# Another order for the side work of the query and key units in an encoder block

## The chip, the core and the metric

The kernel runs on one core of a Trainium2 chip. The time is the device time of one execution in microseconds (us). A core has a matrix engine (TensorE, PE in the profile), three engines for element-wise work (VectorE or DVE, ScalarE or ACT, GpSimd or POOL) and SyncE (SP), whose queue starts most of the transfers here. Each engine works through its own queue in order and waits, where it has to, for semaphores that others set.

## The reference, cut to what matters

One layer of an encoder, all in float32, with 256 tokens and a width of 2048:

```python
h = _rmsnorm(x, norm1_g)
proj = h @ w_in                 # q: 12 heads of 128, k and v: 4 heads of 128, u: 512
a = _rmsnorm(_window_attention(q, k, v, sink), attn_out_g)
f = _rmsnorm(_fourier_mix(u, w_fourier), fourier_out_g)
x = x + jnp.concatenate([a, f], axis=-1) @ w_out
x = x + _conv_ffn(_rmsnorm(x, norm2_g), w_up, dw_w, dw_b, w_down)
return _rmsnorm(x, normf_g)
```

In the attention, a head's scores are `q k^T` times a constant, plus a term that falls with the distance of the two tokens; `m` is the larger of the greatest score and the head's sink, `p = exp(scores - m)` is divided by its sum (with the sink in it), and the result multiplies `v`. Three query heads share one key head.

## The kernel before, in words

**Precision by parts.** Each product is made of three: a float32 operand is split into a high part (`hi`, rounded to the matrix engine's format) and the rest (`lo`). For weights that come from memory, ACT makes `hi` (L181) and DVE makes `lo` (L182), 128 x 2048 numbers at a time. Activations are split in the same way, mostly by `split_scaled` (ACT L269, DVE L270).

**Units.** The work up to the output projection is a row of units, each with one such piece of weights: units 4 to 7 make v, units 8 to 23 make q and k (16 units in groups of four: k, then three q; one has 32 matmuls at L350), units 24 to 39 are the output projection. The function `unit` sets the order in every queue for unit i:

1. `before`: small matmuls of other heads (values L749, turned weights L704, scores L654), on PE ahead of the unit's own;
2. the unit's own matmuls, on PE;
3. `beside`: the side work on ACT, DVE, POOL and SP, the part that is changed;
4. `split(i + 2)`: the split of weights (L181, L182) for the unit after the next, and on SP the load of weights three pieces ahead;
5. `behind`: the exponentials (`exps`, ACT L684 and L688, then a sum on POOL, L689).

Nothing but the order of these calls and the semaphores decides what runs when. In this document "the `lo` of unit i" is the L182 at the end of unit i's side work, which holds weights of unit i + 2.

**The way of a head.** Let a q head be made by unit s. Its steps fall into later units:

- s + 1: `qk_out` reads the two halves of the product from PSUM and adds them (ACT `tmp` L631, DVE `add` L633; for a k, one more DVE step, L635). `qk_parts` splits the sum into the parts `qT` or `kT` (ACT L269 or L643, DVE L270 or L644).
- s + 2: on PE `scores` (L654), first in the unit. Then `scores_out` adds the distances and takes the maxima (DVE L670); POOL makes `neg` out of the maxima in two steps on 128 x 2 numbers (L674, L675). Behind the split, `exps`.
- s + 3: `weigh` divides by the sum (DVE, reciprocal L694, scaling L697), and `flip_out` transposes 32 x 32 blocks (DVE L314) and sends them to memory (SP L317). The last two heads have no flip; PE turns their weights (L704) in s + 4, and `turn_out` splits them (L716, L717).
- s + 4: `flip_in` reads the blocks back in turned order (SP L325).
- s + 6: `flip_parts` splits the turned weights into `pt` (ACT L739, DVE L740, two halves each).
- s + 7 (s + 5 without a flip): on PE `values` (L749), first in the unit; `values_out` squares the head's output (ACT L486), splits it into `cat` (L269, L270) and adds the squares on POOL (L490).

So one unit's side work belongs to as many as five heads. Heads are made only by the q units, so that the work repeats every four units. Counted from unit 8: the first and second unit of a group (16 and 17, 20 and 21) have all steps; the second has a k to sum; the third (18, 22) has no scores and no turned weights to split; the fourth (19, 23) has no scaling, transposition or values.

Of the kernel before, what the change touches and what calls it, by code (L numbers as in the profile page):

```python
# [55 lines left out]
FLIPS = range(NH - 2)  # L56
# [48 lines left out]
def block_kernel(  # L105
# [30 lines left out]
    def bank(pool, name):  # L136
        return pool.tile([P, 512], F32, tag=pool.name, name=name)
# [79 lines left out]
    def u_part(k, o, n, m=1):  # L217

        rows = ux[k // 4][:, (k < 4) * U_HEAD :].rearrange("p (k c) -> p k c", k=4)
        return rows[:, k % 4 : k % 4 + m, o : o + n]  # L220
# [39 lines left out]
    ps = bank(dn, "ps_warm")  # L260
# [112 lines left out]
    before, beside, behind = {}, {}, {}  # L373

    def at(when, i, f, *a):
        when.setdefault(i, []).append((f, a))
# [17 lines left out]
    for k in range(NK):  # L394
# [3 lines left out]
        n = 1 if c < 2 else 2  # L398
# [3 lines left out]
        if q % n == 0:  # L402
            w, h = u_part(k, 0, FW, n), hi[:, q : q + n, :]
# [222 lines left out]
    qk_sb, st = {}, {}  # L626
    sq_a = ph.tile([P, S], F32, tag="sq", name="sq_a")

    def qk_out(kind, h, ps):
        tmp = ph.tile([P, S], F32, tag="tmp", name=f"tmp_{kind}{h}", bufs=2)  # L630
        nc.scalar.activation(tmp, ps[:, S : 2 * S], AF.Copy)  # L631
        add = ph.tile([P, S], F32, tag="add", name=f"add_{kind}{h}", bufs=2)
        nc.vector.tensor_tensor(add, ps[:, 0:S], tmp, ALU.add)  # L633
        if kind == "k":
            nc.vector.tensor_tensor(add, add, r1b, ALU.mult)  # L635
        st["add", kind, h] = add
# [125 lines left out]
    for i in range(N_QK, N_OUT + 8):  # L762
        heads = {i - s: h for (kind, h), s in slot_of.items() if kind == "q"}
        new = [kh for kh, s in slot_of.items() if i - s == 1]
        for n, h in sorted(heads.items()):
            if n == 5 + 2 * (h in FLIPS):
                at(before, i, values, h)
        if 4 in heads and heads[4] not in FLIPS:
            at(before, i, turn, heads[4])
        if 2 in heads:  # L770
            at(before, i, scores, heads[2])
        if 6 in heads and heads[6] in FLIPS:
            at(beside, i, flip_parts, heads[6])
        if 3 in heads:
            at(beside, i, weigh, heads[3])
            if heads[3] in FLIPS:
                at(beside, i, flip_out, heads[3])
        if 4 in heads and heads[4] in FLIPS:
            at(beside, i, flip_in, heads[4])
        for kind, h in new:  # L780
            at(beside, i, lambda k=kind, h=h: qk_out(k, h, st.pop(("ps", k, h))))
        for n, h in sorted(heads.items()):
            if n == 5 + 2 * (h in FLIPS):
                at(beside, i, values_out, h)
        if 4 in heads and heads[4] not in FLIPS:
            at(beside, i, turn_out, heads[4])
        if 2 in heads:
            at(beside, i, scores_out, heads[2])
        for kind, h in new:
            at(beside, i, qk_parts, kind, h)  # L790
        if 2 in heads:
            at(behind, i, exps, heads[2])

# [85 lines left out]
    for n, (c, kq) in enumerate(OUT_ORDER):  # L879
        i = N_OUT + n  # L880
# [14 lines left out]
        if kq >= 2:  # L895
            part = "a" if kq == 2 else "f"
            ps = ps_a[c] if kq < 3 else ps_a[c, "f"]
# [315 lines left out]
    for q in range(2):  # L1213
        kind, j = items[q]
        ps = bank(mm, f"ps_{kind}{j}")
# [15 lines left out]
    for n, it in enumerate(items):  # L1231
# [8 lines left out]
        if it[0] in ("gate", "val"):  # L1240
            kind, j = it
            ps = bank(mm, f"ps_{kind}{j}")
# [4 lines left out]
        if it[0] == "product":  # L1247
            kind, g, c, p = it
# [3 lines left out]
            elif end and p in ("P2", "N4"):  # L1252
                ps = joined[c, p] = bank(mm, f"ps_{p}{g}{c}")
                by_parts(ps, parts[p], *halves.pop(it), GROUPS[g][1], True, False)
            else:
                ps = bank(mm, f"ps_{p}{g}{c}")
# [5 lines left out]
        else:  # L1262
            kind, c = it
            hi, lo = halves.pop(up_index[n])
            if c < 2:
                ps = [joined.pop((c, p)) for p in ("P2", "N4")]
            else:
                ps = [bank(mm, f"ps_l{c}{b}") for b in range(2)]
# [10 lines left out]
    i = up_index[n]  # L1279
# [158 lines left out]
```

## Time and profile before

| | |
|---|---|
| median of 3 runs | 940.92 us (940.85 to 941.05) |
| the profiled execution | 941.03 us, of which span 938.9 us |
| busy: TensorE, DVE, ACT, POOL | 928.0, 765.5, 539.6, 72.9 us |
| mean granted clock of TensorE | 0.997 |
| the q and k units, by TensorE | about 53 to 157 us of the span |

A row of a timeline has the start in us from the span's start, the duration in us, the engine, the line of the kernel, the operation, what it writes from what it reads, and in brackets how long the engine had been idle before it and what released it. A row of the waits has the engine and line that waited, the engine and line waited for, and the total in us, the number of times and the longest. Names have their numbers left out: `lo` is every low part of weights.

### The profile page before, as it was taken

To read this page: it belongs to the slowest core of one execution; us is meant where nothing else is said; L and a number is where in the kernel's file an instruction comes from. 1 tells how busy PE (TensorE), PEld (TensorE's weight loads), DVE (VectorE), ACT (ScalarE), POOL (GpSimd) and SP (SyncE) were. 2 spreads that over 40 slices of the span, in tenths; PEclk is the share of its full clock that TensorE was granted. 3 is DMA by queue.
4 is the path that set the end of the run, shared out by engine and by line. 5 is a ranking of instruction groups with operands and counts; after the bars stand their busy time and mean duration, and the time that the engine had idled before them with its cause. 6 is when DMAs were issued, how large, how long until landed. Compare 5 with 4: busy or idle time off the path is not lost.

```text
span 938.9 us, 12849 instructions
## 1 busy us (share of the span) xinstructions
PE 928.0 (99%) x5005; PEld 803.5 (86%) x5005; DVE 765.5 (82%) x945; ACT 539.6 (57%) x672; POOL 72.9 (8%) x104
## 2 busy tenths in 40 slices
PE   9999999999999999999999999999999999999996
PEld 7888888888888888888888888888888888888885
DVE  7657888778677777798888997878979789989986
ACT  7755666645554555566555665556655556655553
POOL 0102222300000000000000000000000000000002
PEclk9999999999999999999999999999999999999998
DMA  9965767557757668887797778777787978779652
GB/s 367 309 224 169 231 196 236 193 174 281 243 221 232 177 227 238 278 269 239 220 296 252 246 216 286 237 262 232 260 248 240 309 224 269 241 233 273 194 179 90
DMA packets 55148, 223.25 MB, mean 238 GB/s; under 512 B 21136, under 2 KB 25744, under 8 KB 31536
## 3 DMA queue, kind: packets, MB, share of 16 engines
q1 hardware_dynamic: 50544, 192.94, 56.8%
q0 software_dynamic: 4544, 29.49, 16.9%
q8 instruction: 39, 0.64, 0.3%
q14 instruction: 21, 0.17, 0.1%
HBM read 216.13 MB, written 6.29 MB: 237 GB/s over the span
## 4 chain that ended last, share of the span: by engine, by line
PE 95%; DVE 2%; ACT 1%; issue 1%; DMA 0%; POOL 0%; DVEq 0%; POOLq 0%; ACTq 0%
PE ps_val L350 25%; PE ps_gate L350 25%; PE ps_q L350 5%; PE ps_P L1148 3%; PE ps_P L1149 3%; PE ps_P L1147 3%; PE ps_N L1148 3%; PE ps_N L1149 3%; PE ps_N L1147 3%; PE ps_k L350 2%; PE ps_a L333 2%; PE ps_a L335 2%; PE ps_a L334 2%; PE ps_s L654 1%; PE ps_ff L333 1%; PE ps_ff L335 1%
## 5 line engine op out<-in xcount | busy, mean ns | idle before, releaser
L182 DVE TENSOR_TENSOR lo<-raw,hi 128x2048 fp32r<-128x2048 f32 (+1 forms) x129 | 293.5, 2275 | 53.9 <-ACT hi L181 53.6
L181 ACT ACTIVATE hi<-raw 128x2048 fp32r<-128x2048 f32 (+1 forms) x129 | 245.3, 1902 | 36.7 <-PE ps_a L334 14.6
L350 PE MATMUL ps_val<-hU,hi 128*128 128x512 f32 x688 | 236.2, 389 | 0.0
L350 PE MATMUL ps_gate<-hU,hi 128*128 128x512 f32 x688 | 236.2, 389 | 0.0
L350 PE MATMUL ps_val<-hU,lo 128*128 128x256 f32 x688 | 189.9, 276 | 0.0
L350 PE MATMUL ps_gate<-hU,lo 128*128 128x256 f32 x688 | 189.9, 276 | 0.0
L350 PEld LDWEIGHTS ps_gate<-hU,hi 128*128 128x128 f32 x688 | 129.1, 188 | 26.8
L350 PEld LDWEIGHTS ps_val<-hU,hi 128*128 128x128 f32 x688 | 129.1, 188 | 26.8
L350 PEld LDWEIGHTS ps_gate<-hU,lo 128*128 128x128 f32 x688 | 129.1, 188 | 1.3
L350 PEld LDWEIGHTS ps_val<-hU,lo 128*128 128x128 f32 x688 | 129.1, 188 | 1.3
L922 ACT ACTIVATE ft_g<-ps_gate 128x256 f32<-128x256 f32 x43 | 16.5, 384 | 123.0 <-PE ps_gate L350 123.0
L922 ACT ACTIVATE ft_v<-ps_val 128x256 f32<-128x256 f32 x43 | 16.5, 384 | 91.5 <-PE ps_val L350 91.5
L350 PE MATMUL ps_q<-hT,hi 128*128 128x512 f32 x192 | 65.1, 391 | 0.0
L1147 PE MATMUL ps_P<-hi_P,op_P 128*128 128x512 f32 x144 | 56.0, 389 | 0.0
L1148 PE MATMUL ps_P<-hi_P,op_P 128*128 128x512 f32 x144 | 56.0, 389 | 0.0
L1149 PE MATMUL ps_P<-lo_P,op_P 128*128 128x512 f32 x144 | 56.0, 389 | 0.0
L350 PE MATMUL ps_q<-hT,lo 128*128 128x256 f32 x192 | 51.2, 277 | 0.0
L1039 DVE TENSOR_TENSOR lo_N<-sumw,hi_N 128x2048 fp32r<-128x2048 f32 (+1 forms) x20 | 41.5, 2077 | 9.4 <-ACT hi_N L1038 9.2
L1147 PE MATMUL ps_N<-hi_N,op_N 128*128 128x512 f32 x108 | 42.0, 389 | 0.0
L1148 PE MATMUL ps_N<-hi_N,op_N 128*128 128x512 f32 x108 | 42.0, 389 | 0.0
L1149 PE MATMUL ps_N<-lo_N,op_N 128*128 128x512 f32 x108 | 42.0, 389 | 0.0
L350 PEld LDWEIGHTS ps_q<-hT,hi 128*128 128x128 f32 x192 | 35.2, 188 | 6.6
(389 smaller groups left out, 1598.9 us busy)
## 6 DMA issues: line engine op xcount, KB each, us to landing
raw<-in_w_up SPq DMA_DIRECT2D x86, 1024.0 KB, 5.6
raw<-in_w_in SPq DMA_DIRECT2D x20, 1024.0 KB, 5.3
raw<-in_w_out SPq DMA_DIRECT2D x16, 1024.0 KB, 4.9
sumw<-in_w_down POOLq DMA_DIRECT2D x16, 1024.0 KB, 8.7
raw<-in_w_down_late SPq DMA_DIRECT2D x4, 1024.0 KB, 7.0
raw<-in_w_down_last SPq DMA_DIRECT2D x4, 768.0 KB, 4.2
turnp<-flip SPq DMA_DIRECT2D x40, 64.0 KB, 2.9
flop<-turnp SPq DMA_DIRECT2D x10, 256.0 KB, 4.7
```

The lines of the kernel that those rows point to most:

```text
L181: nc.scalar.activation(hi[:, 0:n], raw[:, 0:n], AF.Copy)
L182: nc.vector.tensor_tensor(lo[:, 0:n], raw[:, 0:n], f32(hi[:, 0:n]), ALU.subtract)
L333: nc.tensor.matmul(ps, ah, wh, start=first and q == q0, stop=False)
L334: nc.tensor.matmul(ps, al, wh, start=False, stop=False)
L335: nc.tensor.matmul(ps, ah, wl, start=False, stop=last and q == q0 + len(kk) - 1)
L350: nc.tensor.matmul(ps[:, x], (hi, lo)[i][:, k * P : (k + 1) * P], hk(k)[:, x], start=n == 0 and k == 0, stop=n == len(order) - 1 and k == ...
L654: nc.tensor.matmul(ps[:, b * S : (b + 1) * S], qT[:, qo + b * P : qo + (b + 1) * P], kT[:, ko : ko + S], start=n == 0, stop=n == 2,)
L922: nc.scalar.activation(tmp, ps[:, S : 2 * S], AF.Copy)
L1039: nc.vector.tensor_tensor(lo, src, f32(hi), ALU.subtract)
L1147: nc.tensor.matmul(ps, o[:, 0, p, :], hi[:, s], start=first and p == 0, stop=False)
L1148: nc.tensor.matmul(ps, o[:, 1, p, :], hi[:, s], start=False, stop=False)
L1149: nc.tensor.matmul(ps, o[:, 0, p, :], lo[:, s], start=False, stop=last and p == n - 1)
```

## The change

Before, the order of a unit's `beside` was: turned weights split, scaling and transposition, transposed blocks read back, sum of the new q or k, a head's output, (turned weights of the last two heads,) scores, parts of the new q or k. After, it is: sum of the new q or k, turned weights split, its parts, a head's output, scaling and transposition, transposed blocks read back or turned weights of the last two heads, scores. On each engine the queue holds the same instructions as before in the new order; the split of weights and the exponentials still follow. In units without a new q or k (25 on) only a head's output changes its place, to stand ahead of the scaling.

```diff
         if 2 in heads:
             at(before, i, scores, heads[2])
+        for kind, h in new:
+            at(beside, i, lambda k=kind, h=h: qk_out(k, h, st.pop(("ps", k, h))))
         if 6 in heads and heads[6] in FLIPS:
             at(beside, i, flip_parts, heads[6])
+        for kind, h in new:
+            at(beside, i, qk_parts, kind, h)
+        for n, h in sorted(heads.items()):
+            if n == 5 + 2 * (h in FLIPS):
+                at(beside, i, values_out, h)
         if 3 in heads:
             at(beside, i, weigh, heads[3])
             if heads[3] in FLIPS:
                 at(beside, i, flip_out, heads[3])
-        if 4 in heads and heads[4] in FLIPS:
-            at(beside, i, flip_in, heads[4])
-        for kind, h in new:
-            at(beside, i, lambda k=kind, h=h: qk_out(k, h, st.pop(("ps", k, h))))
-        for n, h in sorted(heads.items()):
-            if n == 5 + 2 * (h in FLIPS):
-                at(beside, i, values_out, h)
-        if 4 in heads and heads[4] not in FLIPS:
-            at(beside, i, turn_out, heads[4])
+        if 4 in heads:
+            at(beside, i, flip_in if heads[4] in FLIPS else turn_out, heads[4])
         if 2 in heads:
             at(beside, i, scores_out, heads[2])
-        for kind, h in new:
-            at(beside, i, qk_parts, kind, h)
         if 2 in heads:
             at(behind, i, exps, heads[2])
```

## The prediction

> **What bounds the kernel now.** I read the page's busy times first, then the waits of TensorE, then the timelines of the stretch that the change touches.
>
> ```profile
> span 938.9 us, 12849 instructions
> PE 928.0 (99%) x5005; PEld 803.5 (86%) x5005; DVE 765.5 (82%) x945; ACT 539.6 (57%) x672; POOL 72.9 (8%) x104
> ```
> ```profile
> PE ps_s L654 <- ACT qT L269: 1.4, 2, 0.9
> ```
>
> TensorE is busy for 99% of the span, so it sets the time. Only its own waits can be won back, and any new wait on it counts in full. Of its waits, one line is in the stretch of the change: twice the scores (L654) waited for the q parts (`qT`), 1.4 us in all. The places, and the two others that I need later:
>
> ```profile
> 122.94 1.19 PE L654 MATMUL ps_s<-kT,qT 128*128 128x256 f32 x6 [0.54 <-ACT qT L269]
> 130.16 0.88 PE L654 MATMUL ps_s<-kT,qT 128*128 128x256 f32 x6
> 150.43 1.20 PE L654 MATMUL ps_s<-kT,qT 128*128 128x256 f32 x6 [0.85 <-ACT qT L269]
> 177.39 0.40 PE L749 MATMUL ps_o<-pt,v_hi 128*128 128x256 f32 x2
> ```
>
> Besides the idle 0.54 and 0.85 us, the two waiting groups of scores are stretched by 0.31 and 0.32 against the free one at 130.16 (0.88). All that can be won is 2.0 us. The waits lie 27.49 us apart, which is four units: the side work of VectorE (DVE) and ScalarE (ACT) is a loop that runs slightly slower than TensorE, and TensorE catches up with it once in a group of four.
>
> How that loop turns (units 20 to 23; a unit's split of weights, `lo` at L182, is the mark from which I count):
>
> ```profile
> 103.11 2.29 DVE L182 TENSOR_TENSOR lo<-raw,hi 128x2048 fp32r<-128x2048 f32 x1 [1.27 <-ACT hi L181]
> 106.19 0.62 DVE L697 TENSOR_SCALAR sc<-sc,ex 128x256 f32<-128x256 f32 x2
> 117.93 2.29 DVE L182 TENSOR_TENSOR lo<-raw,hi 128x2048 fp32r<-128x2048 f32 x1 [0.87 <-ACT hi L181]
> ...
> 130.31 2.29 DVE L182 TENSOR_TENSOR lo<-raw,hi 128x2048 fp32r<-128x2048 f32 x1 [1.27 <-ACT hi L181]
> 132.52 0.75 DVE L740 TENSOR_TENSOR pt<-flop,pt 128x256 fp32r<-128x256 f32 x2
> 133.19 0.16 DVE L694 RECIPROCAL ex<-sm 128x2 f32<-128x2 f32 x1
> 133.38 0.90 DVE L697 TENSOR_SCALAR sc<-sc,ex 128x256 f32<-128x256 f32 x2
> ...
> 134.95 0.39 DVE L633 TENSOR_TENSOR add_q<-ps_q,tmp_q 128x256 f32<-128x256 f32 x1
> 135.26 0.47 DVE L270 SCALAR_TENSOR_TENSOR cat<-ps_o,vec,cat 128x256 fp32r<-128x256 f32 x1
> 135.65 0.41 DVE L670 CUSTOM_DVE_ANT_0 sc<-ps_s,rel 128x256 f32<-128x256 f32 x1
> 136.33 0.42 DVE L270 SCALAR_TENSOR_TENSOR qT<-add_q,qT 128x256 fp32r<-128x256 f32 x1
> 137.63 2.29 DVE L182 TENSOR_TENSOR lo<-raw,hi 128x2048 fp32r<-128x2048 f32 x1 [0.88 <-ACT hi L181]
> ...
> 142.70 0.42 DVE L635 TENSOR_TENSOR add_k<-add_k,r1b 128x256 f32<-128x256 f32 x1
> 145.41 2.29 DVE L182 TENSOR_TENSOR lo<-raw,hi 128x2048 fp32r<-128x2048 f32 x1 [0.87 <-ACT hi L181]
> 152.21 2.29 DVE L182 TENSOR_TENSOR lo<-raw,hi 128x2048 fp32r<-128x2048 f32 x1 [1.38 <-ACT hi L181]
> 155.09 0.42 DVE L633 TENSOR_TENSOR add_q<-ps_q,tmp_q 128x256 f32<-128x256 f32 x1
> 157.80 2.29 DVE L182 TENSOR_TENSOR lo<-raw,hi 128x2048 fp32r<-128x2048 f32 x1 [1.27 <-ACT hi L181]
> ```
> ```profile
> 122.47 0.42 ACT L269 ACTIVATE qT<-add_q 128x256 fp32r<-128x256 f32 x1 [2.32 <-DVE add_q L633]
> ...
> 131.54 0.71 ACT L739 ACTIVATE pt<-flop 128x256 fp32r<-128x256 f32 x2
> ...
> 135.38 0.42 ACT L269 ACTIVATE qT<-add_q 128x256 fp32r<-128x256 f32 x1 [2.23 <-DVE add_q L633]
> 135.70 1.90 ACT L181 ACTIVATE hi<-raw 128x2048 fp32r<-128x2048 f32 x1
> ```
>
> DVE does the turned weights, the scaling and the transposition before `add_q`; ACT stands still for 2.2 to 2.3 us until `add_q` is there, then does `qT` and `hi`; and DVE, done with everything, waits 0.9 to 1.4 us for that `hi` before `lo`. Four units take 7.32 (unit 20), 7.78 (21, a k unit), 6.80 (22, no scores) and 5.59 us (23, no scaling), 27.49 in all.
>
> **What the change removes.** With `add_q` first, ACT no longer waits for it so long, `hi` comes earlier, and the idle time before `lo` goes. That shortens the DVE part. No instruction is added or dropped; the queues of PE, SP and POOL keep their order; the transposition's DMAs move later with it, but their result is read only three units on, so I cost them at nothing; if that cover were gone, TensorE's values would wait for `pt`.
>
> **What the change adds.** The idle time before `lo` was in use. After the scores, GpSimd (POOL) makes `neg` out of the maxima in two tiny steps, and ACT's exponentials need it. One unit of the kernel before, 25, has no q or k to sum, so its `hi` is early and its `lo` follows the scores at once. That is what nearly every unit with scores will now look like:
>
> ```profile
> 165.11 2.29 DVE L182 TENSOR_TENSOR lo<-raw,hi 128x2048 fp32r<-128x2048 f32 x1 [0.88 <-ACT hi L181]
> 170.34 2.29 DVE L182 TENSOR_TENSOR lo<-raw,hi 128x2048 fp32r<-128x2048 f32 x1
> 176.38 0.67 DVE L717 TENSOR_TENSOR pt<-ps_t,pt 128x512 fp32r<-128x512 f32 x1
> ```
> ```profile
> 136.50 0.31 POOL L674 TENSOR_TENSOR neg<-mx,rq_neg 128x2 f32<-128x2 f32 x1 [2.62 <-DVE mx L670]
> 136.90 0.28 POOL L675 TENSOR_SCALAR neg<-neg,sink_neg 128x2 f32<-128x2 f32 x1
> 170.50 2.18 POOL L674 TENSOR_TENSOR neg<-mx,rq_neg 128x2 f32<-128x2 f32 x1 [2.17 <-DVE mx L670]
> 172.78 0.28 POOL L675 TENSOR_SCALAR neg<-neg,sink_neg 128x2 f32<-128x2 f32 x1
> ```
> ```profile
> 173.10 0.60 ACT L684 ACTIVATE sc<-sc,neg,rq_pos 128x256 f32<-128x256 f32 x1 [3.61 <-POOL neg L675]
> 174.47 0.36 ACT L486 ACTIVATE sq<-ps_o 128x256 f32<-128x256 f32 x1
> 174.73 0.46 ACT L269 ACTIVATE cat<-ps_o,vec 128x256 fp32r<-128x256 f32 x1
> ```
>
> The first `neg`, 0.31 us otherwise, took 2.18 and ended 0.05 after `lo` ended (172.63): POOL is shut out while DVE runs its split. ACT gets past the exponentials only at 174.47, 4.13 after `lo` began. In the new order the next thing on ACT is `tmp_q`, and the first thing on DVE, `add_q`, needs it: at 4.13 + 0.36 + 0.03 (the usual hand-over) = 4.52 after `lo`, where DVE would be free at 2.21 (130.31 to 132.52). Behind `add_q` all of DVE's queue stands still for 2.31 us. Before, the scaling and transposition of another head filled this time.
>
> When does it happen? Counted from `add_q`: ACT starts `qT` at 0.43, the next step 0.32 later, Square 0.26 and `cat` 0.46: done at 1.47; `hi` starts about 0.1 earlier and is ready at about 3.3. DVE starts its `cat` at 1.50, then cat 0.39, reciprocal 0.19, scaling and transposition 1.57 (133.38 to 134.95) with a 0.90 scaling, or 1.29 with the 0.62 one at 106.19, scores 0.68: `lo` could start at 4.05 to 4.33. `hi` is there 0.8 us before, so units 16, 17, 20, 21 and 24 are caught. In a unit 15, 19 or 23, `lo` still waits for `hi` (2.71 after `add_q`), and POOL should just get by.
>
> **The sum**, from `lo` to `lo`, with the 0.62 scaling:
> - like 20: 2.21 + 4.05 = 6.26 (before 7.32).
> - like 21: 4.52 + 4.05 + 0.42 for the second k step (142.70) = 8.99 (7.78).
> - like 22: 4.52 + 4.05 - 0.68 = 7.89 (6.80).
> - like 23: 2.21 + 2.71 = 4.92 (5.59).
>
> A group takes 28.06 where it took 27.49, all of it behind scores that TensorE already waits for. Three places:
> 1. Scores at 122.94. `qT` is ready at 5.37 (4.52 + 0.43 + 0.42) after the `lo` of 117.93, no earlier than before (4.96), though it now stands ahead of everything. From the `lo` at 103.11: 6.26 + 8.99 + 5.37 = 20.62 against 19.78, +0.84. I take that `lo` itself as unmoved: the first groups' gains and blocks about cancel (an estimate from the same periods).
> 2. Scores at 150.43: one group more, +0.57.
> 3. Values at 177.39, which need the `pt` of 176.38 (ready 177.05, so 0.34 to spare). From the scores' start, 0.05 after `qT`, unit 22 has more left to its `lo`: 7.89 - 5.42 = 2.47, before 1.78 (150.43 to 152.21), +0.69; unit 23 -0.67; unit 24 6.26 against 7.31, -1.05; unit 25 comes behind 24's late exponentials, its `cat` at 4.13 + 0.71 + 0.26 + 0.46 + 0.03 = 5.59 (0.71 for two turned halves on ACT, 131.54) and, with cat 0.39, reciprocal 0.19, scaling 0.65 and scores 0.68, `lo` at 7.50 against 5.23, +2.27. Together +1.24, less the slack: +0.90.
>
> That is +2.3 us. With the 0.90 scaling in six units from 17 on, 0.28 each, it is +4.0. The 0.90 stood where POOL's sum of squares ran beside it; in the new order that sum begins some 0.9 us before the scaling and mostly ends first, so the truth lies between, and I take +3.1. The profiled execution was 941.03 us (its span 938.9 and 2.1 around it), against a median of 940.92; the sum goes on the median: 944.0 us, 943.2 to 944.9 by the two rows, 942.8 to 945.3 with 0.4 either way for the `lo` taken as unmoved.
>
> **The rivals.**
> *The blocked step reaches units 15, 19 and 23 too.* There the second `neg` starts about 2.65 after `add_q` (0.31 + 0.67 + 0.42 for sum, turned weights and q's parts, 0.85 from scores to `neg`, 0.40 more; some 0.1 less where these overlap), and `lo` at 2.71: a lead of 0.05 to 0.2 us for a step of 0.28. This speaks for it:
>
> ```profile
> 74.33 0.58 POOL L675 TENSOR_SCALAR neg<-neg,sink_neg 128x2 f32<-128x2 f32 x1
> 74.35 0.48 DVE L270 SCALAR_TENSOR_TENSOR cat<-y,vec,cat 128x256 fp32r<-128x256 f32 x1 [0.17 <-ACT cat L269]
> ```
>
> POOL's step began 0.02 earlier and still ran to the end of DVE's. If a longer lead is worth no more, the exponentials start 2.38 after `lo`, `add_q` comes at 2.38 + 1.37 + 0.39 = 4.14 instead of 2.21, in units 16, 20 and 24: 5.8 us more, 949.8. The Trainium skill (SBUF — State Buffer, Who interferes with whom) says that whichever of the two issues first keeps the shared port for the whole instruction; by that rule POOL wins here, this rival falls, and the sum stays at 944.0. The row at 74.33 does not bear the rule out for so short a lead.
>
> *Faster: nothing is blocked.* If `hi` comes over 0.85 us after the scores (136.33 to 137.18, the end of both `neg` steps) or the port is free, every unit follows its shorter DVE part; four of them take 23.4 us (28.06 less 2.31 twice), less than TensorE's own 26.3 (27.49 less 0.85 and 0.32), and both waits go: 2.0 us less, 938.9. Against it stands 170.50, and that `hi` has 0.8 us in hand.
>
> *About the same.* The blocks cost what I say, but the early `qT` leaves the first groups a lead and the values at 177.39 do not wait: terms 1 and 3 vanish, 941.5.
>
> **How the numbers follow.** Forecast 0.48, the wider block 0.27, about the same 0.13, nothing blocked 0.12. A difference within 0.2% (1.9 us) can hardly be told from none: slower by more than that 0.76, same 0.13, faster 0.11. The range 941.0 to 950.5 leaves out the faster case and little else; the likeliest case's own range is 942.8 to 945.3.
>
> **What would show it.** Right: `neg` at L674 at about 2.2 us in units 16, 17, 20, 21, 24 and 25; `tmp_q` or `tmp_k` late by waits of ACT's exponentials for `neg`; DVE idle about 2.3 us before `add_q`; scores still waiting for `qT`, and values for `pt` near 177. The wider block shows as L675 at about 2 us in units 15, 19 and 23. Wrong: no wait at L654 at all, or `lo` still starting after `neg`.

## The result, and the profile after

| | before | after |
|---|---|---|
| median (14 runs of each) | 941.24 us (940.85 to 942.23) | 943.12 us (942.82 to 944.53) |
| the profiled execution, its span | 941.03 us, 938.9 us | 943.75 us, 942.0 us |
| mean granted clock of TensorE | 0.997 | 0.997 |

The changed kernel is slower by 1.9 us, a ratio of 1.0021 with a 95% interval of 1.0013 to 1.0029. I had predicted 944.0, within 941.0 to 950.5.

A part of the time lies outside the profile's span: some 2.1 us in the kernel before (2.08 to 2.20 in its runs beside the experiments), some 1.75 in the changed one (1.73 to 1.86). So the span grew by some 0.35 us more than the time. Of the kernels below only the one with the scores last has the longer rest; all others have 1.72 to 1.85, as the changed one. What sets it, no run shows.

The first lines of the page after:

```profile
span 942.0 us, 12850 instructions
PE 928.3 (99%) x5005; PEld 802.7 (85%) x5005; DVE 762.7 (81%) x945; ACT 540.7 (57%) x672; POOL 80.7 (9%) x104
```

TensorE is busy for as long as before (928.0) in a longer span, so it waits more; POOL is busy for 7.8 us more with the same instructions, and DVE for 2.8 less. TensorE's waits after (engine and line that waits, what for: total us, times, longest):

```profile
PE ps_s L654 <- ACT qT L269: 3.6, 3, 1.5
PE ps_o L749 <- DVE pt L717: 0.5, 1, 0.5
```

Before there were 1.4 us, twice. Their places after, in TensorE's timeline (the second row stops at the edge of its view; the whole group of six takes 1.20 us, as the others do):

```profile
96.97 1.20 PE L654 MATMUL ps_s<-kT,qT 128*128 128x256 f32 x6 [1.17 <-ACT qT L269]
124.51 0.84 PE L654 MATMUL ps_s<-kT,qT 128*128 128x256 f32 x3 [0.91 <-ACT qT L269]
152.68 1.20 PE L654 MATMUL ps_s<-kT,qT 128*128 128x256 f32 x6 [1.54 <-ACT qT L269]
180.38 0.39 PE L749 MATMUL ps_o<-pt,v_hi 128*128 128x256 f32 x1 [0.46 <-DVE pt L717]
```

The scores at 122.94 and 150.43 start 1.57 and 2.25 later, the values at 177.39 start 2.99 later, and one group waits that did not before. Its row in the kernel before has no bracket:

```profile
95.73 1.21 PE L654 MATMUL ps_s<-kT,qT 128*128 128x256 f32 x6
```

Why the parts are late is seen on the other engines. DVE after, from the `lo` of unit 15 to that of unit 19 (without the steps between):

```profile
103.72 2.29 DVE L182 TENSOR_TENSOR lo<-raw,hi 128x2048 fp32r<-128x2048 f32 x1 [0.60 <-ACT hi L181]
110.01 2.29 DVE L182 TENSOR_TENSOR lo<-raw,hi 128x2048 fp32r<-128x2048 f32 x1
114.53 0.42 DVE L633 TENSOR_TENSOR add_k<-ps_k,tmp_k 128x256 f32<-128x256 f32 x1 [2.23 <-ACT tmp_k L631]
119.07 2.29 DVE L182 TENSOR_TENSOR lo<-raw,hi 128x2048 fp32r<-128x2048 f32 x1
123.58 0.42 DVE L633 TENSOR_TENSOR add_q<-ps_q,tmp_q 128x256 f32<-128x256 f32 x1 [2.23 <-ACT tmp_q L631]
127.01 2.25 DVE L182 TENSOR_TENSOR lo<-raw,hi 128x2048 fp32r<-128x2048 f32 x1
131.88 2.29 DVE L182 TENSOR_TENSOR lo<-raw,hi 128x2048 fp32r<-128x2048 f32 x1 [0.61 <-ACT hi L181]
```

POOL in units 16 and 19, and ACT behind the split of unit 16:

```profile
110.17 2.18 POOL L674 TENSOR_TENSOR neg<-mx,rq_neg 128x2 f32<-128x2 f32 x1 [4.10 <-DVE mx L670]
112.44 0.28 POOL L675 TENSOR_SCALAR neg<-neg,sink_neg 128x2 f32<-128x2 f32 x1
...
131.36 0.20 POOL L674 TENSOR_TENSOR neg<-mx,rq_neg 128x2 f32<-128x2 f32 x1 [5.82 <-DVE mx L670]
131.65 0.29 POOL L675 TENSOR_SCALAR neg<-neg,sink_neg 128x2 f32<-128x2 f32 x1
```
```profile
112.76 0.60 ACT L684 ACTIVATE sc<-sc,neg,rq_pos 128x256 f32<-128x256 f32 x1 [3.52 <-POOL neg L675]
114.13 0.36 ACT L631 ACTIVATE tmp_k<-ps_k 128x256 f32<-128x256 f32 x1
```

The `lo` at 110.01 follows the scores without a gap. The `neg` that starts 0.16 us behind it takes 2.18 us instead of 0.31 and ends at 112.35, 0.05 after `lo` (112.30). ACT stands before the exponentials for 3.52 us, so `tmp_k`, next in its queue, is late; and DVE, whose first step needs it, waits 2.23 us and adds at 114.53, 4.52 after its `lo`. In unit 19 the second step starts 0.23 ahead of `lo` (131.65 against 131.88) and gets by. The waits of ACT between 75 and 180 us, after:

```profile
ACT sc L684 <- POOL neg L675: 26.7, 8, 3.5
ACT qT L269 <- DVE add_q L633: 9.2, 10, 1.9
```

and before:

```profile
ACT qT L269 <- DVE add_q L633: 24.2, 10, 3.0
```

The change took 15 us of waiting for `add_q` off ACT, as it was to do, and put 26.7 us of waiting for POOL in its place.

### The profile page after: what moved, and what is told of

Its sections match the earlier page's. It is cut to its first block, busy times and chain, and to the rows that moved or that the text cites. A ratio compares the mean times of both kernels' runs of the same rounds, so it can differ in the third digit from the quotient of the medians.

```text
span 942.0 us, 12850 instructions
## 1 busy us (share of the span) xinstructions
PE 928.3 (99%) x5005; PEld 802.7 (85%) x5005; DVE 762.7 (81%) x945; ACT 540.7 (57%) x672; POOL 80.7 (9%) x104
## 3 DMA queue, kind: packets, MB, share of 16 engines
HBM read 216.13 MB, written 6.29 MB: 236 GB/s over the span
## 4 chain that ended last, share of the span: by engine, by line
PE 76%; DVE 7%; ACT 5%; DMA 5%; issue 4%; POOL 2%; SPq 0%; DVEq 0%; POOLq 0%; ACTq 0%
PE ps_val L350 25%; PE ps_gate L350 25%; PE ps_P L1145 3%; PE ps_P L1146 3%; PE ps_P L1147 3%; PE ps_N L1145 3%; PE ps_N L1146 3%; PE ps_N L1147 3%; DVE lo L182 2%; ACT hi L181 2%; PE ps_a L335 2%; PE ps_a L333 2%; PE ps_a L334 2%; POOL neg L674 2%; DMA chan<-in_c_chan 2%
```

## The experiments

The theory: a `lo` that follows the scores at once shuts POOL out, and ACT's and DVE's queues stand still behind it. The rivals: the new order is slow for other reasons; or the parts of the edit cost what they cost one by one. Each ratio is to runs of the kernel before on the same chip (median 941.28 us for the first four, then 941.01 for four, 941.52 for three, 941.10 for the last). In these ratios every kernel but the one with the scores last has the 0.35 us outside the span in its favour; differences to the changed kernel don't contain it.

| kernel | median us | ratio to before, 95% interval |
|---|---|---|
| after, `neg` on DVE | 937.92 | 0.9964 [0.9952, 0.9977] |
| after, scores ahead of scaling | 938.31 | 0.9967 [0.9954, 0.9979] |
| after, four copies behind the scores | 938.19 | 0.9968 [0.9956, 0.9981] |
| after, old order from unit 24 | 942.76 | 1.0019 [1.0010, 1.0028] |
| before, `neg` on DVE | 941.29 | 1.0002 [0.9993, 1.0011] |
| before, sum first, nothing else | 941.22 | 1.0003 [0.9994, 1.0011] |
| before, scores last, nothing else | 941.07 | 1.0004 [0.9995, 1.0013] |
| before, four copies | 942.87 | 1.0022 [1.0012, 1.0031] |
| after, one copy | 943.23 | 1.0018 [1.0009, 1.0026] |
| after, two copies | 944.07 | 1.0025 [1.0014, 1.0036] |
| after, once more | 943.52 | 1.0026 [1.0015, 1.0038] |
| after, three copies | 938.19 | 0.9968 [0.9957, 0.9980] |

**`neg` on DVE**, in the changed kernel and, as the control, in the kernel before:

```diff
-        nc.gpsimd.tensor_tensor(neg, mx, rq_neg, ALU.mult)
-        nc.gpsimd.tensor_scalar(neg, neg, sink_neg[:, h : h + 1], None, ALU.min)
+        nc.vector.tensor_tensor(neg, mx, rq_neg, ALU.mult)
+        nc.vector.tensor_scalar(neg, neg, sink_neg[:, h : h + 1], None, ALU.min)
```

> The changed order, with both steps that make neg (L674, L675) on DVE instead of POOL; nothing else. Theory (POOL is shut out by DVE's split, and ACT's exponentials and then tmp queue behind it): the two steps stand ahead of lo on DVE and cost some 0.2 to 0.5 us there, the exponentials no longer wait 3.5 us, add_q starts about 2.2 after lo instead of 4.5 in the units behind 16, 17, 20, 21 and 24, a group takes 24 to 26 us, TensorE's waits for qT and pt go: about 938.5 to 939.5 us, some 2 below the kernel before and 4 below the changed one. Rival (the sum or the scaling in its new place is what is late, not neg): the waits at L654 stay, 943.

> The kernel before, with the two small steps that make `neg` on DVE instead of POOL: the control to the same edit on the changed kernel, which gained 5.2 us. The theory (in the changed kernel POOL was shut out by `lo`): in the old order `lo` waits for `hi` 0.9 to 1.4 us after the scores, `neg` is done by then on either engine and DVE has the 0.4 us to spare before `lo`, so nothing is won: 941.3, between 940.5 and 942.0, the scores' two waits still there. Rival (the step is simply better on DVE, whatever the order): about 938, faster than before by some 3 us.

The changed kernel with `neg` on DVE takes 937.92 us, 5.2 less than with it on POOL, though two instructions are added to DVE's queue in each of the 12 units with scores. DVE at the end of unit 16 and the start of 17:

```profile
106.84 0.23 DVE L675 TENSOR_SCALAR neg<-neg,sink_neg 128x2 f32<-128x2 f32 x1
106.98 2.28 DVE L182 TENSOR_TENSOR lo<-raw,hi 128x2048 fp32r<-128x2048 f32 x1
109.26 0.42 DVE L633 TENSOR_TENSOR add_k<-ps_k,tmp_k 128x256 f32<-128x256 f32 x1
```

`add_k` follows 2.28 after `lo` instead of 4.52, and TensorE has no wait from 55 to 200 us. In the kernel before the same edit wins nothing: the waits for `qT` stay at 1.3 us, twice, and the median span is 939.5 us against 938.9 of the kernel before. So `neg` is not better on DVE as such; it is POOL's place in the new order that costs.

**The scores ahead of the scaling**, in the changed kernel: the call of `scores_out` moved up, with scaling and transposition between it and `lo`.

```diff
+        if 2 in heads:
+            at(beside, i, scores_out, heads[2])
         if 3 in heads:
             at(beside, i, weigh, heads[3])
...
-        if 2 in heads:
-            at(beside, i, scores_out, heads[2])
```

> The changed order, but scores_out moved ahead of the scaling and transposition (sum, turned weights, parts, a head's output, scores, scaling and transposition, read back). No operation is added. Theory: neg has the scaling and transposition (about 1.3 us) before lo begins and is not shut out (0.2 and 0.3 us), the exponentials follow hi at once, a group takes less than TensorE's own 26.3 us, and all waits go: 938.5 to 939.5 us. Rival (the sum first is what costs): 943. Second rival (POOL is shut out by the scaling too): neg at 0.9 us or so, the gain shrinks to 940.

938.31 us, and no wait of TensorE. On POOL L674 takes 210 ns in the mean and L675 377, L675 being 0.42 where it runs beside the scaling. This is the same work as in the changed kernel in yet another order, faster than both.

**Useless copies behind the scores**, four, then the control, then one, two and three:

```diff
+        fill = ph.tile([P, P], F32, tag="fill", name=f"fill{h}")
+        for _ in range(4):
+            nc.vector.tensor_copy(fill, ps[:, 0:P])
```

> The changed order with work added that computes nothing: behind the scores DVE copies a quarter of the scores' PSUM bank four times into a scratch tile, some 0.7 us, before its split. Theory: POOL makes neg during the copies, the exponentials start about when lo starts, and the 2.2 us wait before add_q goes: 0.7 us more work in 12 units makes the kernel faster than the changed one, by 3 to 4 us, 939 to 940. Rival (the time is DVE's work and not the block): 0.6 to 0.7 us more in each of some 5 units that count, 944 to 947.

> The kernel before with the same four useless copies behind the scores on DVE (1.26 us in each of the 12 units) that made the changed kernel 5 us faster: the control. In the old order `neg` had its time already. The theory: 1.26 us stands against 0.87 to 1.38 us of DVE's waiting for `hi`, so 0.4 us are lost in about half of the units with scores, some 1 us in all: 942.2, between 941.2 and 943.5. Rival (the copies help for another reason, by other timing on TensorE or on transfers): below 940.

> The changed kernel with one useless copy (about 0.31 us on DVE) behind the scores, where four made it 5 us faster. In the changed kernel the two `neg` steps start 0.16 and 0.46 us after the `lo` that shuts them out. One copy lets the first start 0.15 us ahead of `lo`, the second 0.15 after it. The theory (one step shut out costs nearly as much as two): `neg` at L674 about 0.2, at L675 about 2.2 us; `add` at 4.23 after `lo` instead of 4.52, twice in a group, against two copies of 0.31: no change, 943.1, between 942.3 and 944.0, the scores' waits still there. Rival (time lost falls in proportion to the steps let through): about 941.

> The same with two copies (about 0.64 us): both steps start ahead of `lo`, the second by some 0.18 us for a step of 0.28. The theory (a step that starts 0.2 us ahead keeps POOL's way to memory, as in unit 23 of the changed kernel): nothing is shut out, a group takes about 25.1 us, less than TensorE's 26.3, no waits: 938.3, between 937.5 and 939.2. Rival (the step must be finished before `lo` starts): L675 at about 2.2 us, 943.5 or more, slower than the changed kernel.

> The changed kernel with three useless copies (about 0.95 us), between the two that cost 0.5 us or more and the four that gained 5. With two copies the second `neg` step started 0.08 us ahead of `lo` and was still held to its end; with three it starts some 0.38 us ahead and is done (0.28) before `lo` begins. The theory (all that matters is whether both steps get through): a jump, as with four copies: 938.3, between 937.5 and 939.2, L675 at 0.28, no waits of the scores. Rival (each copy counts by itself, and four worked by their sum): between 940 and 943.

Four copies, 1.27 us of DVE's time in each unit with scores (I had expected 0.7), make the changed kernel 4.9 us faster. In the kernel before they cost 1.9, where I had expected some 1: TensorE there also waits for DVE's `qT`, which the copies hold up (1.3 us, 3 times). The smaller numbers show why: the time is not a sum over copies. One copy, POOL and DVE in units 16 and 17:

```profile
109.50 0.19 POOL L674 TENSOR_TENSOR neg<-mx,rq_neg 128x2 f32<-128x2 f32 x1 [4.11 <-DVE mx L670]
109.79 2.19 POOL L675 TENSOR_SCALAR neg<-neg,sink_neg 128x2 f32<-128x2 f32 x1
```
```profile
109.54 2.30 DVE L182 TENSOR_TENSOR lo<-raw,hi 128x2048 fp32r<-128x2048 f32 x1
113.78 0.42 DVE L633 TENSOR_TENSOR add_k<-ps_k,tmp_k 128x256 f32<-128x256 f32 x1 [1.95 <-ACT tmp_k L631]
```

The first step is through, the second is shut out, and `add_k` comes 4.24 after `lo` instead of 4.52: 0.28 won, 0.3 paid for the copy, 943.23. Two copies, units 16 and 19:

```profile
109.40 2.42 POOL L675 TENSOR_SCALAR neg<-neg,sink_neg 128x2 f32<-128x2 f32 x1
...
130.91 0.28 POOL L675 TENSOR_SCALAR neg<-neg,sink_neg 128x2 f32<-128x2 f32 x1
```
```profile
109.48 2.29 DVE L182 TENSOR_TENSOR lo<-raw,hi 128x2048 fp32r<-128x2048 f32 x1
...
131.14 2.29 DVE L182 TENSOR_TENSOR lo<-raw,hi 128x2048 fp32r<-128x2048 f32 x1
```

Here my expectation fell and its rival stood: I had counted on a lead of some 0.18 us for the second step in unit 16; it was 0.08, and the step was held for 2.42 us, to 0.05 after `lo` (the same in units 17, 20 and 21). The kernel is no faster than the changed one beside it (944.07 and 943.52). In unit 19, where the lead is 0.23, the step took 0.28. The rival's form of it, that the step must be finished before `lo` starts, falls there: it ended 0.05 into it. Three copies, unit 16 and the start of 17:

```profile
107.69 0.28 POOL L675 TENSOR_SCALAR neg<-neg,sink_neg 128x2 f32<-128x2 f32 x1
```
```profile
108.09 2.28 DVE L182 TENSOR_TENSOR lo<-raw,hi 128x2048 fp32r<-128x2048 f32 x1
110.29 0.42 DVE L633 TENSOR_TENSOR add_k<-ps_k,tmp_k 128x256 f32<-128x256 f32 x1
```

Both steps are through, `add_k` follows 2.20 after `lo`, and the time jumps from 944.07 to 938.19, the same as with four. Added work makes a kernel 5 us faster, and all of the gain comes between the second and the third copy, where the second step gets through. Together with the two repairs that add no copies, this leaves none of the named rivals.

**One part of the change alone**, in the kernel before: the sum first; or the scores behind the parts.

```diff
+        for kind, h in new:
+            at(beside, i, lambda k=kind, h=h: qk_out(k, h, st.pop(("ps", k, h))))
         if 6 in heads and heads[6] in FLIPS:
             at(beside, i, flip_parts, heads[6])
...
-        for kind, h in new:
-            at(beside, i, lambda k=kind, h=h: qk_out(k, h, st.pop(("ps", k, h))))
```

> The kernel before with one part of the change alone: the sum of q or k moved to the front, while the new parts stay behind the scores. ACT's `hi` is still early, so `lo` follows the parts at once; but the parts' DVE step (0.42 us) now stands between the scores and `lo`, so the first `neg` step gets through and only the second is shut out. The theory, by hand from the rows of before: a group of four units takes about 6.1 + 8.4 + 6.9 + 4.9 = 26.3 us, no more than TensorE's own 26.3, so most of the scores' waits go: 939.3, between 938.0 and 940.5. Rival (the block costs as much as in the changed order): 943.

```diff
-        if 2 in heads:
-            at(beside, i, scores_out, heads[2])
         for kind, h in new:
             at(beside, i, qk_parts, kind, h)
+        if 2 in heads:
+            at(beside, i, scores_out, heads[2])
```

> The kernel before with the other part of the change alone: the scores moved behind the new parts, the sum as late as before. `hi` still comes 2.7 us after the sum and `lo` waits for it, by when `neg` is through. The theory: unchanged, 941.3, between 940.5 and 942.2; `neg` at 0.2 to 0.3 us in the q and k units. Rival (scores last are enough to have POOL shut out): 943, with `neg` at 2.2 us.

The scores last changed nothing, as expected: L674 takes 228 ns in the mean up to unit 24, L675 287, and the waits are those of before. The sum first was to gain 2 us and gained none (941.22; its median span is 939.4 us against 938.9). POOL behaved as I had said (L674 0.31, L675 2.20 us, held from 107.42 on), but my count of the period was short: from the `lo` of 107.19 to that of 134.65 a group takes 27.46 us, not 26.3. In the k unit (17) it took 9.12 us, where I had counted 8.4. There DVE's two halves of the turned weights took 1.29 us instead of 0.75, with POOL's sum of squares beside them:

```profile
112.23 1.29 DVE L740 TENSOR_TENSOR pt<-flop,pt 128x256 fp32r<-128x256 f32 x2
```
```profile
112.35 0.90 POOL L490 TENSOR_TENSOR sq_a<-sq_a,sq 128x256 f32<-128x256 f32 x1 [0.94 <-ACT sq L486]
```

ACT had its halves done at 112.00, so they were not what DVE waited for. The scaling took 0.93 and 0.90 us in units 18 and 20 instead of 0.62, again beside POOL's sums. Together this is 1.1 of the 1.16 us that my count was short. And TensorE's wait changed its name:

```profile
PE ps_s L654 <- DVE qT L270: 1.7, 2, 1.0
```

ACT's part is early now, DVE's part still stands behind the scores, and TensorE waits for that. So two things on POOL take back what the earlier sum wins: the second step shut out (`add_k` at 111.42, 4.23 after its `lo`), and the sums of squares that stretch DVE's steps. No run has the one without the other.

**The old order from unit 24 on** (`N_OUT` is 24; the two orders stand as comments here), and **the changed kernel once more**:

```diff
+        if i < N_OUT:
             # the order of the changed kernel
+        else:
+            # the order of the kernel before
```

> The changed order up to unit 23, the order of before from unit 24 on. Theory (term 3 of the forecast): in unit 24 neg is no longer shut out, values at unit 27 do not wait for pt (0.46 us of idle, 0.74 with the late end), and the waits for qT stay as in the changed kernel: 0.7 us below the changed kernel, about 942.4. Rival (what is won there is lost at a later step of the side work): no difference, 943.1.

> The changed kernel once more, beside the two others: 943.1 by its earlier runs; every theory expects the same, and the side loop's first `lo` in the q and k units shows whether the 0.55 us by which it began later in the profiled execution belongs to the kernel or to that one execution.

With the old order from 24 on TensorE's wait for `pt` is gone; the one for `qT` stays (3.1 us, 3 times). The median is 0.4 us below the 943.12 of the changed kernel and its lowest run 0.7 below (942.15 against 942.82): the sign is right, the size is within the scatter. Its own profile can't give the size: the granted clock (behind the busy time and count of TensorE) fell to 0.56 and 0.58 for 4 us in it, some 1.7 us of lost work.

```profile
154.00:156.00 2.00, 2.00 (x9) 0.56 0.17 54
156.00:158.00 2.00, 2.00 (x9) 0.58 0.61 99
```

The second run of the changed kernel tells apart what the first one's profile mixed. The `lo` of unit 10, two units ahead of the first one that shuts POOL out, in the kernel before, after, and after once more (here with the first scores that wait):

```profile
70.06 2.29 DVE L182 TENSOR_TENSOR lo<-raw,hi 128x2048 fp32r<-128x2048 f32 x1 [1.40 <-ACT hi L181]
```
```profile
70.61 2.29 DVE L182 TENSOR_TENSOR lo<-raw,hi 128x2048 fp32r<-128x2048 f32 x1 [1.41 <-ACT hi L181]
```
```profile
70.33 2.29 DVE L182 TENSOR_TENSOR lo<-raw,hi 128x2048 fp32r<-128x2048 f32 x1 [1.40 <-ACT hi L181]
96.71 1.20 PE L654 MATMUL ps_s<-kT,qT 128*128 128x256 f32 x6 [0.59 <-ACT qT L269]
```

The first profile's loop began 0.55 us late, the second's 0.27; the scores at 96 us start 0.26 earlier with it (96.97, 96.71). Its time is that of the first (943.46 and 943.75), and in the kernel with one copy, which shares the new order, that `lo` stands at 69.88, ahead of the kernel before. So the late start belongs to the execution, not to the change.

## Why the prediction was right, and where not

- **What bounds the kernel, and what was to be won.** Right: without the block TensorE has no wait between 55 and 200 us, in four kernels. The price was too low. I took 2.0 us; the four won 2.9 to 3.4, of which 0.35 outside the span. The scores at 95.73 (1.21 us, shown above) were a third stretched group, 0.33 over the free 0.88, that I passed over for its want of a bracket. The other 0.2 to 0.7 us are not explained. The first three repairs also came out 0.2 to 0.8 us below the ranges that I had expected of them.
- **What the change adds.** Right in each step: `neg` 2.18 us, ending 0.05 after `lo`, exponentials late, `tmp` late, the sum 4.52 after `lo`. The units caught are 16, 17, 20, 21, 24 and 25, as named, and units 15, 19 and 23 get by. In the first group units 12 and 13 are caught as well (2.20 us for L675, 2.18 for L674).
- **The periods.** 6.29, 9.06, 7.94 and 4.87 us for units like 20 to 23 (103.72, 110.01, 119.07, 127.01, 131.88 above), forecast 6.26, 8.99, 7.89 and 4.92; a group 28.16, forecast 28.06.
- **The terms.** From the `lo` of unit 15 (103.11 before, 103.72 after) to the scores that need unit 18's parts (122.94 and 124.51) the loop took 0.96 us longer than before, predicted 0.84; the next group 0.68 more, predicted 0.57; the values 0.74 more, predicted 0.90. Together 2.38, and 2.3 was the sum by the 0.62 scaling. Of the profile's 3.1 us of span 0.61 more are for the `lo` at 103.72, which I had taken as unmoved (within 0.4); 0.55 of this is the late start, 0.06 the change (in the second profile 0.35, of which 0.27).
- **The terms that were mis-sized** are in the last step of the sum, where I took +3.1 from between 2.3 and 4.0. The 0.90 scaling does not occur: all twelve are at 0.61 or 0.62 in the new order, since POOL's sum of squares ends first, in unit 17 at 117.02, 0.1 before the scaling. The group of the scaling over 60 to 180 us, before and after:

```profile
L697 DVE TENSOR_SCALAR sc<-sc,ex 128x256 f32<-128x256 f32 x24 | 9.4, 433 | 0.4
```
```profile
L697 DVE TENSOR_SCALAR sc<-sc,ex 128x256 f32<-128x256 f32 x24 | 7.4, 351 | 0.4
```

 So the span should have grown by 2.3 us, and it did: by 2.38 in the three terms of the profile, and by 2.3 in the medians of the later runs (941.7 against 939.4). The second term is the 2.1 us around the span, which I took as unmoved without a reason; they fell to some 1.75. That is why the time grew by 1.9 to 2.0 only. The 0.62 end of my sum, 943.2, lies beside the measured 943.12 by some luck: the kernel before stood at 941.24 in the runs beside the changed one and not at 940.92, which makes up for the 0.35. That the first profile's span grew by 3.1, the very number that I took, is chance: a term too many stands against the late start.
- **The wider block** fell: a lead of 0.23 us is enough, in the changed kernel and in the one with two copies. But it was nearer than I had thought, for with 0.08 the step is held. In the prediction I had set the Trainium skill (SBUF — State Buffer, Who interferes with whom) against the row at 74.33: whichever of the two issues first keeps the port. By the recorded starts this holds for unit 19 and does not hold for a lead of 0.08 in the kernel with two copies, where the measured hold decides. Whether the page's rule fails there, or a recorded start 0.08 us earlier is not an earlier issue, no run shows.
- **Nothing blocked** fell for the change, and is what its three repairs do. **About the same** fell in its mechanism: the values at 177.39 do wait. In size it lay close: the difference of 0.2% is at the edge of what I had called no change.

## What to carry to other kernels

An idle time in front of an instruction may be in use by another engine: before an edit closes it, look for who works in it, and what that engine's result holds up in the next queue. Where the result is urgent and tiny, put it on the engine that runs next, or leave other useful work between it and the long instruction; here either turned a loss of 1.9 us into a gain of some 3. Whether a step is held up is a matter of tenths of a microsecond and all or nothing, so half a remedy (one copy, two copies) brings nothing. And the engine that was let in can slow its neighbour in turn, as POOL's sums of squares did in the kernel with the sum first.

## What was not expected of the hardware

How much lead POOL needs differs between the two steps. L675 was held with 0.08 us and free with 0.23; L674 was free with 0.04 (109.50 against the `lo` of 109.54, one copy; the same in six more units). And POOL can shut DVE out too. In the kernel with the sum first, POOL's sum of squares began 0.02 us before `lo` by the record:

```profile
83.17 0.74 POOL L490 TENSOR_TENSOR sq_f<-sq_f,sq 128x256 f32<-128x256 f32 x1
```
```profile
83.19 2.87 DVE L182 TENSOR_TENSOR lo<-raw,hi 128x2048 fp32r<-128x2048 f32 x1
```

There `lo` took 2.87 us instead of 2.29, 0.58 more. The Trainium skill says on the same page and section that the two contend when DVE's instruction has two inputs in SBUF and GpSimd's reads SBUF, and not when DVE's has at most one and runs outside the modes with two ports. The copies from PSUM agree with this, since beside three of them L674 and L675 took 0.20 and 0.28 us.
